# Eight rooms for expert weights, earlier rows of x, and six expert pairs combined by one-hot products

## The chip, the core and the metric

The kernel runs on one core of a Trainium2 chip. The metric is the device time of one execution in microseconds. All times inside an execution are counted from the start of the profiled span.

## What is computed

Two transformer blocks run one behind the other on 512 tokens of width 1024, in float32. The change lies in the second half of the first block, a mixture of 32 experts, and in the out projection in front of it:

```python
x = x + merged @ w_out
h2 = rmsnorm(x, norm2_g)
# router: best of 4 groups, then the best 2 of its 8 experts, gates from two softmaxes
# each token goes to 2 experts:
hid = silu(xb @ w_gate[e]) * (xb @ w_up[e])      # 1024 -> 256, twice
y   = (hid @ w_down[e]) * gate                   # 256 -> 1024
x = x + sum over the token's two experts of y
```

All 32 experts' weights (100.7 MB) have to be read from memory once.

## The kernel before

**Stages.** `window` computes the first block's mixer and, in `outproj`, the new x, block of 128 features by block (`X[:, d]`, d = 0 to 7). `moe` does the experts. `l0`, `ffn`, `l1`, `ffn` are the second block. Each engine works through its instructions in the order in which they were written.

**Rows.** The experts gather tokens by row, so x has to be in memory as rows (`hrows`). `Moe.row` (line 1683) turns one feature block by four TensorE transposes, copies it on ScalarE and writes 256 KB from ScalarE's queue. For d below `DROWS` (4) this is done in the out projection, a few matmuls behind the block; for the others in `route` (line 1709), in front of the routing's small matrix products.

**Pairs.** The experts are handled in 16 pairs (`NP`), 64 slots for each expert, 128 rows for a pair. A pair p takes: `gather` of its rows by POOL, `turn` (line 1888: eight transposes, then VectorE's multiplication by the gain), `gu` (line 1900: 32 matmuls from two weight pieces of 2 MB each, the gate and up products), `turn_hid`, and `down` (line 1926: 16 matmuls from a third piece). The loop runs `gu` of pair p and then `down` of pair o = p - 1.

**Combining.** Pairs below `NS` (12) are scattered: `down` writes one copy times the gate, `scatter` (line 1859) writes its rows to `yrows` in memory from POOL, and when the last of them has been written, `results` reads `yrows` back in four blocks of 128 tokens (1 MB each), two blocks at first and two when those have been added. `add_results` (line 1874) sums the two expert rows of each token on VectorE, transposes the sums on TensorE and adds them to X; it runs in the iterations o = 12 and o = 13, two blocks in each. The other four pairs are combined by one-hot products: `down` writes a copy and a correction to it (two operands), `spread` (line 1946) writes a matrix C with a one where token and slot meet, and `comb` (line 1951) multiplies, two pairs at a time, four matmuls of 128x512 for each d, and adds to X on VectorE. Pairs 12 and 13 are combined in pieces of two d in the iterations of pairs 14 and 15, pairs 14 and 15 in the last stage (`lastcomb`, lines 2136 on), between the first matmuls of `l0`.

**Rooms.** A weight piece is loaded into a room as soon as the room is free and its turn has come; `moe_jobs` (line 1581) writes down which piece goes into which room, `Core._dma` (line 90) issues, from SP's queue. Rooms are: ring 2, the two slabs (`esH`, `esL`); ring 1, two tiles `ew`; ring 0, `raw`; ring 3, one tile `ey`; ring 4, four `t` tiles of 256 KB; ring 5, the split-weight tiles `wh` and `wl`, four each; ring 6, two tiles of 512 KB. Five pieces are issued in the out projection, one at the start of `moe`, and three from ScalarE's queue behind the gates. In the steady state seven rooms turn round.

Of the kernel before, what the change touches and what calls it, by code (L numbers as in the profile page):

```python
# [8 lines left out]
F32 = mybir.dt.float32  # L9
F32R = mybir.dt.float32r  # L10
# [28 lines left out]
class Core:  # L39


    def __init__(self, ctx, tc, aps):
        self.tc, self.nc, self.a = tc, tc.nc, aps
        self.ctx = ctx
        self.const = ctx.enter_context(tc.tile_pool(name="const", bufs=1))
        self.slab = ctx.enter_context(tc.tile_pool(name="slab", bufs=1))
        self.wp = ctx.enter_context(tc.tile_pool(name="wp", bufs=1))
        self.xs = ctx.enter_context(tc.tile_pool(name="xs", bufs=1, side="right"))
        self.wr = ctx.enter_context(tc.tile_pool(name="wr", bufs=1, side="right"))
        self.tmp = ctx.enter_context(tc.tile_pool(name="tmp", bufs=1, side="right"))  # L50
        self.ps = ctx.enter_context(tc.tile_pool(name="ps", bufs=1, space=bass.MemoryType.PSUM))
        self.dram = ctx.enter_context(tc.tile_pool(name="dr", bufs=1, space=bass.MemoryType.DRAM))
        self.jobs = []
        self.groups = []
        self.n_dma = 0
        raw = lambda: self.wr.tile([128, 2048], F32, name="raw", tag="raw", bufs=NRAW)
        self.rings = [[raw, NRAW, 0], None, None, None, None, None, None]
        self.n_split = 0
        self.cur = 0
        self.turns = 0  # L60
        self.now = 0
        self.blk_off = 0
# [1511 lines left out]
NP = 16  # L1574
CAP = 64
NI = 12
NS = 12
DROWS = 4


def moe_jobs(c):

    gs = {}
    order = moe_order()

    def piece(i, *ring):
        n = order[i]
        w = c.a["e_w"][n // 3]
        o = 2 * (n % 3)
        if len(ring) == 1:  # L1590
            gs[n] = c.add_job(w[o:o + 2].rearrange("e p n -> p e n"), [(4096, 1)], split=False, ring=ring[0])
        else:
            gs[n] = sum((c.add_job(w[o + e], [(2048, 1)], split=False, ring=ring[e]) for e in range(2)), [])

    rooms = [(2,), (3,), (2,), (1,), (1,), (0, 0), (0, 4)]
    piece(0, 2)
    piece(4, 2)
    yield
    for i, ring in ((5, (1,)), (6, (1,)), (7, (0, 0)), (2, (6, 6)), (1, (5, 5)), (3, (3,)), (8, (0, 4))):
        piece(i, *ring)  # L1600
    for i in range(9, len(order)):
        ring = rooms.pop(0)
        if ring == (3,) and i > order.index(3 * NS + 3):
            ring = rooms.pop(0)
        rooms.append(ring)
        piece(i, *ring)
    for n in order:
        c.groups += gs[n]
    yield
# [13 lines left out]
class Moe:  # L1623
# [319 lines left out]
            nc.scalar.activation(Y[0][:, sl], acc, AF.Copy, scale=gate)  # L1943
            nc.vector.scalar_tensor_tensor(Y[1][:, sl], acc, gate, Y[0][:, sl], op0=OP.mult, op1=OP.subtract)

    def spread(self, idc, last):
        C = self.c.t512(F32R) if last else self.c.wp.tile([128, T], F32R, name="C", tag="wh", bufs=NSPL)
        self.c.nc.vector.tensor_scalar(C, self.iota, idc, None, op0=OP.is_equal)
        return C

    def comb(self, X, d, slots):
# [56 lines left out]

        return self.pool2.tile([128, 4096], F32, name="ey", tag="y0")

    def quarters(self):
        return Row([self.pool2.tile([128, D], F32, name="eq", tag="yq", bufs=4) for _ in range(2)])


def moe(c, X, nn, next_g):
    nc = c.nc
    c.mark("moe")
    m = c.moe
    m.pool2 = c.pool(m.es, "moe2")
    c.rings[3] = [m.early, 1, 0]  # L2020
    c.rings[6] = [m.quarters, 2, 0]
    c._dma()
    m.route(X)

# [12 lines left out]

    gather = lambda p: m.gather(m.idg[:, p:p + 1], p)
    xg = {}
    for p in range(2):  # L2040
        onehot(p, 1)
        slots(p)
        xg[p] = gather(p)
    m.gates()
    c.rings[4] = [lambda: Row([c.t512() for _ in range(4)]), 1, 0]
    turns = iter(("wh", "wl"))

    def halves():
        tag = next(turns)
        return Row([c.wp.tile([128, SPL], F32, name="we", tag=tag, bufs=NSPL) for _ in range(4)])  # L2050

    c.rings[5] = [halves, 2, 0]
    c._dma(queue=nc.scalar)
    xt = {0: m.turn(xg.pop(0))}
    slots2(0)
    slots2(1)
    C = {}
    Y = {}
    held = []

    def w():

        release()
        j, r = c.take_raw()
# [11 lines left out]
    comb = lambda q, d: m.comb(X, d, [(Y[q], C[q]), (Y[q + 1], C[q + 1])])  # L2076
    c.mark("experts")
    onehot(2)
    ht = {}
    for p in range(NP + 1):  # L2080
        if p < NP:
            hd = m.gu(xt.pop(p), w, m.rs[:, p:p + 1])
            release()
        if p == 0:
            slots(2)
            slots2(2)
        if p + 2 < NP:
            xg[p + 2] = gather(p + 2)
        if p + 1 < NP and p < 1:
            xt[p + 1] = m.turn(xg.pop(p + 1))  # L2090
        o = p - 1
        q = (o // 2 - 1) * 2
        ds = [] if q < NS else list(range(4)) if o % 2 == 0 else list(range(4, 8))
        for d in ds[:2]:
            comb(q, d)
        if o >= 0:
            tile = lambda dt: m.pool2.tile([128, D], dt, name="y", tag="yq", bufs=4)
            if o == NS:
                y = m.pool2.tile([128, 4, D], F32R, name="y4", tag="y0")
            if o < NS:  # L2100
                Y[o] = (tile(F32),)
            elif o < NP - 2:
                Y[o] = (y[:, 2 * (o - NS)], y[:, 2 * (o - NS) + 1])
            else:
                Y[o] = (tile(F32R), tile(F32R))
            m.down(ht.pop(o), w(), m.gate[:, o:o + 1], Y[o])
            release()
            if o < NS:
                m.scatter(o, Y[o][0])
            if o == NS - 1:  # L2110
                rooms = (lambda: Row([c.wp.tile([128, SPL], F32, name="yr", tag="wh", bufs=NSPL) for _ in range(4)]),
                         lambda: Row([tile(F32), tile(F32)]))
                res = [m.results(i, rooms[i]()) for i in range(2)]
            if o >= NP - 2:
                C[o] = m.spread(m.idc[:, o:o + 1], True)
        if 1 <= p < NP - 1:
            xt[p + 1] = m.turn(xg.pop(p + 1))
        for d in ds[2:]:
            comb(q, d)
        if p < NP:  # L2120
            ht[p] = m.turn_hid(hd)
        if o in (NS, NS + 1):
            b = 2 * (o - NS)
            for i in range(2):
                m.add_results(X, b + i, res[i])
            if o == NS:
                res = [m.results(2 + i, rooms[i]()) for i in range(2)]
            else:
                for q in (NS, NS + 1):
                    C[q] = m.spread(m.idc[:, q:q + 1], False)  # L2130
        if 1 <= p < 7:
            slots(2 * p + 2)
            slots2(2 * p + 2)
        if p < 6:
            onehot(2 * p + 4)
    m.beyond(X)
    c.mark("lastcomb")
    nn = c.norm_begin(next_g)
    accs = [c.bank(), c.bank()]
    c._split(c.cur + 1)  # L2140
    c._lows()
    for d in range(NB + 2):
        if d < NB:
            comb(NP - 2, d)
        if 1 <= d <= NB:
            nn[3](d - 1, X[:, d - 1])
            nc.sync.dma_start(c.xdr[:, d - 1], X[:, d - 1])
        if d >= 2:
            for acc in accs:
                for _ in c.block(1, *nn[:2], acc, first=d == 2, last=d == NB + 1, x0=d - 2):  # L2150
                    pass
    m.es.close()
    return nn[:3], accs
# [169 lines left out]
```

## Time and profile before

| | us |
|---|---|
| median of three runs | 1871.73 (1870.38 to 1872.22) |
| the profiled execution | 1871.83 |
| its span | 1870.0 |
| TensorE busy in the span | 1777.3 (95%) |
| VectorE busy | 1041.5 (56%) |
| ScalarE busy | 718.8 (38%) |
| POOL busy | 359.4 (19%) |

The busy shares are means over stages that have different limits; the stretch from about 290 to 650 us is the one that the change touches, and it is to be read by itself. In the rows below, PE is TensorE's matmuls, PEld its weight loads, DVE is VectorE, ACT is ScalarE, and SPq and ACTq are DMA issues from SyncE's and ScalarE's queues. An arrow in brackets names what ended the idle time in front of an instruction.

### The profile page before, as it was taken

To read this page: it belongs to the slowest core of one execution; us is meant where nothing else is said; L and a number is where in the kernel's file an instruction comes from. 1 tells how busy PE (TensorE), PEld (TensorE's weight loads), DVE (VectorE), ACT (ScalarE), POOL (GpSimd) and SP (SyncE) were. 2 spreads that over 40 slices of the span, in tenths; PEclk is the share of its full clock that TensorE was granted. 3 is DMA by queue.
4 is the path that set the end of the run, shared out by engine and by line. 5 is a ranking of instruction groups with operands and counts; after the bars stand their busy time and mean duration, and the time that the engine had idled before them with its cause. 6 is when DMAs were issued, how large, how long until landed. Compare 5 with 4: busy or idle time off the path is not lost.

```text
span 1870.0 us, 23372 instructions
## 1 busy us (share of the span) xinstructions
PE 1777.3 (95%) x8722; PEld 1326.1 (71%) x8722; DVE 1041.5 (56%) x1915; ACT 718.8 (38%) x1418; POOL 359.4 (19%) x392
## 2 busy tenths in 40 slices
PE   8999999799786999999999999999999999999998
PEld 6777787533233686667888888878777788888887
DVE  5765446543113767765655555564776565555555
ACT  6444334211000456664433333333666443333334
POOL 3212012111111251001211111121444221111111
PEclk9999999799997999999999999999999999999999
DMA  6124346599999320202322322243221322222321
GB/s 246 68 65 162 135 156 236 186 399 421 422 422 416 99 94 26 77 29 85 113 90 91 112 90 91 104 127 119 76 60 57 103 100 96 107 90 92 111 91 46
DMA packets 71831, 266.99 MB, mean 143 GB/s; under 512 B 24561, under 2 KB 31089, under 8 KB 46752
## 3 DMA queue, kind: packets, MB, share of 16 engines
q1 hardware_dynamic: 55120, 229.51, 33.2%
q0 software_dynamic: 9936, 27.47, 4.3%
q10 hardware_dynamic: 6656, 8.45, 1.3%
q8 instruction: 72, 1.18, 0.3%
q14 instruction: 47, 0.39, 0.1%
HBM read 251.57 MB, written 18.87 MB: 145 GB/s over the span
## 4 chain that ended last, share of the span: by engine, by line
PE 56%; DVE 6%; ACT 3%; issue 1%; DMA 0%; POOL 0%; POOLq 0%; DVEq 0%; ACTq 0%
PE psacc L227 15%; PE psacc L229 15%; PE psacc L228 15%; PE psT L709 2%; PE psO L861 2%; DVE wl L134 1%; PE psT L341 1%; PE psO L1440 1%; PE psS L1497 1%; PE psS L227 1%; PE psS L1185 1%; ACT wh L125 1%; PE psS L228 1%; PE psS L229 1%; ACT p L696 1%
## 5 line engine op out<-in xcount | busy, mean ns | idle before, releaser
L134 DVE TENSOR_TENSOR wl<-raw,wh 128x512 fp32r<-128x512 f32 x466 | 402.7, 867 | 246.3 <-ACT wh L125 244.8
L227 PE MATMUL psacc<-xh,wh 128*128 128x512 f32 x1008 | 407.4, 404 | 6.6 <-ACT wh L125 6.0
L125 ACT CAST wh<-raw 128x512 fp32r<-128x512 f32 x466 | 285.5, 617 | 321.6 <-PE psacc L228 272.4
L228 PE MATMUL psacc<-xl,wh 128*128 128x512 f32 x1008 | 394.6, 391 | 1.6 <-DVE xl L251 1.6
L229 PE MATMUL psacc<-xh,wl 128*128 128x512 f32 x1008 | 394.7, 392 | 0.1
L227 PEld LDWEIGHTS psacc<-xh,wh 128*128 128x128 f32 x1008 | 190.0, 189 | 56.0 <-issue 14.2
L229 PEld LDWEIGHTS psacc<-xh,wl 128*128 128x128 f32 x1008 | 189.8, 188 | 41.5 <-DVE wl L134 0.6
L228 PEld LDWEIGHTS psacc<-xl,wh 128*128 128x128 f32 x1008 | 190.3, 189 | 35.7 <-DVE xl L251 3.2
L227 PE MATMUL psacc<-uh,wh 128*128 128x512 f32 x480 | 187.0, 390 | 2.6 <-DVE x L453 2.6
L229 PE MATMUL psacc<-uh,wl 128*128 128x512 f32 x480 | 186.8, 389 | 0.0
L228 PE MATMUL psacc<-ul,wh 128*128 128x512 f32 x480 | 186.7, 389 | 0.0
L421 POOL TENSOR_TENSOR t<-t,rstd 128x512 f32<-128x512 f32 x64 | 82.9, 1295 | 526.6 <-ACT t L420 526.6
L453 DVE TENSOR_TENSOR x<-psacc,x 128x512 f32<-128x512 f32 x120 | 82.7, 689 | 125.4 <-PE psacc L229 125.4
L227 PEld LDWEIGHTS psacc<-uh,wh 128*128 128x128 f32 x480 | 90.1, 188 | 22.3 <-issue 3.8
L379 POOL TENSOR_TENSOR ss<-ss,t 128x512 f32<-128x512 f32 (+1 forms) x49 | 58.5, 1193 | 234.9 <-ACT t L372 234.6
L229 PEld LDWEIGHTS psacc<-uh,wl 128*128 128x128 f32 x480 | 90.1, 188 | 18.9
L228 PEld LDWEIGHTS psacc<-ul,wh 128*128 128x128 f32 x480 | 90.1, 188 | 18.5
L243 ACT CAST uh<-t 128x512 fp32r<-128x512 f32 x64 | 39.7, 621 | 131.3 <-DVE t L422 131.3
L709 PE MATMUL psT<-cst,p 128*128 128x128 f32 x448 | 77.1, 277 | 13.4 <-ACT p L696 12.6
L709 PEld LDWEIGHTS psT<-cst,p 128*128 128x128 f32 x448 | 55.2, 140 | 42.6 <-ACT p L696 22.6
L420 ACT ACTIVATE t<-psacc 128x512 f32<-128x512 f32 x64 | 38.3, 599 | 80.8 <-PE psacc L229 80.8
L1914 DVE SCALAR_TENSOR_TENSOR hd<-psS,rs,sl 128x256 f32<-128x256 f32 x16 | 7.7, 484 | 107.9 <-ACT sl L1913 107.9
(493 smaller groups left out, 2707.7 us busy)
## 6 DMA issues: line engine op xcount, KB each, us to landing
raw<-ffn SPq DMA_DIRECT2D x64, 1024.0 KB
ew<-e_w SPq DMA_DIRECT2D x14, 2048.0 KB
raw<-e_w SPq DMA_DIRECT2D x17, 1024.0 KB
esH<-e_w SPq DMA_DIRECT2D x7, 2048.0 KB
esL<-e_w SPq DMA_DIRECT2D x7, 2048.0 KB
ey<-e_w SPq DMA_DIRECT2D x5, 2048.0 KB
raw<-w_in_a SPq DMA_DIRECT2D x8, 1024.0 KB
raw<-od_qk SPq DMA_DIRECT2D x8, 1024.0 KB
```

The lines of the kernel that those rows point to most:

```text
L125: nc.scalar.copy(h[:, :n], r)
L134: self.nc.vector.tensor_sub(l, r, h)
L227: nc.tensor.matmul(acc, wh, xh, start=first, stop=False)
L228: nc.tensor.matmul(acc, wh, xl, start=False, stop=False)
L229: nc.tensor.matmul(acc, wl, xh, start=False, stop=last)
L243: nc.scalar.copy(h, src)
L379: self.nc.gpsimd.tensor_add(s, s, q)
L420: nc.scalar.activation(r, acc, AF.Relu)
L421: nc.gpsimd.tensor_mul(r2, r, st["r2"])
L453: nc.vector.tensor_add(X[:, d], acc, X[:, d])
L709: nc.tensor.transpose(t[:, o:o + 128], p[:, m * 128:m * 128 + 128], c.ident)
L861: self.c.nc.tensor.matmul(o[64 * hh:64 * hh + 64], self.V[:, kb, v:v + 64], pt[hh][:, kb], start=kb == 0, stop=kb == 3, skip_group_check=True)
```

## The change

- `moe_jobs` has eight rooms that turn round. New are a ring of four `wh` tiles with one of two 512 KB tiles `yw` (rings 7 and 6), used up to the piece of pair 9's down product; ring 3 is used up to pair 11's second piece. Each room that consists of quarters or halves is issued as four or two DMAs.
- Five pieces are issued in the out projection as before, and at the start of `moe` two (pieces 1 and 6 of the order) where there was one. Two are issued from ScalarE's queue behind the gates where there were three.
- `DROWS` is 7: the rows of d = 4, 5 and 6 are turned and written in the out projection, d = 7 alone in `route`.
- `NS` is 10. The reads of the results start behind pair 9, `add_results` runs at o = 11 and o = 13. Pairs 10 to 15 are combined by one-hot products: 10 and 11 in front of `down` of pair 12, 12 and 13 in front of `down` of pair 14, each with all eight d in one go; 14 alone in front of `down` of pair 15; 15 alone in `lastcomb`.
- `spread` is called directly behind `down` of each of these pairs, and writes into the tiles `rstd` and `ss`, or a `t` tile for the last two.

```diff
-        self.rings = [[raw, NRAW, 0], None, None, None, None, None, None]
+        self.rings = [[raw, NRAW, 0], None, None, None, None, None, None, None, None]
-NS = 12
-DROWS = 4
+NS = 10
+DROWS = 7
 def moe_jobs(c):
-    rooms = [(2,), (3,), (2,), (1,), (1,), (0, 0), (0, 4)]
+    rooms = [(2,), (2,), (1,), (1,), (0, 0), (7, 6), (3,), (0, 4)]
+    last = {(7, 6): order.index(3 * NS - 1), (3,): order.index(3 * NS + 4)}
     piece(0, 2)
-    piece(4, 2)
+    piece(2, 2)
     yield
-    for i, ring in ((5, (1,)), (6, (1,)), (7, (0, 0)), (2, (6, 6)), (1, (5, 5)), (3, (3,)), (8, (0, 4))):
+    for i, ring in ((3, (1,)), (4, (1,)), (5, (0, 0)), (1, (8, 5)), (6, (7, 6)), (7, (3,)), (8, (0, 4))):
         piece(i, *ring)
     for i in range(9, len(order)):
-        ring = rooms.pop(0)
-        if ring == (3,) and i > order.index(3 * NS + 3):
-            ring = rooms.pop(0)
-        rooms.append(ring)
-        piece(i, *ring)
+        while i > last.get(rooms[0], i):
+            rooms.pop(0)
+        rooms.append(rooms.pop(0))
+        piece(i, *rooms[-1])
...
-    def spread(self, idc, last):
-        C = self.c.t512(F32R) if last else self.c.wp.tile([128, T], F32R, name="C", tag="wh", bufs=NSPL)
-        self.c.nc.vector.tensor_scalar(C, self.iota, idc, None, op0=OP.is_equal)
+    def spread(self, p):
+        c = self.c
+        C = c.t512(F32R) if p >= NP - 2 else c.tmp.tile([128, T], F32R, name="C", tag=("rstd", "ss")[p % 2], bufs=1)
+        c.nc.vector.tensor_scalar(C, self.iota, self.idc[:, p:p + 1], None, op0=OP.is_equal)
         return C
...
 def moe(c, X, nn, next_g):
-    c.rings[3] = [m.early, 1, 0]
-    c.rings[6] = [m.quarters, 2, 0]
+    quarters = lambda tag: Row([c.wp.tile([128, SPL], F32, name="we", tag=tag, bufs=NSPL) for _ in range(4)])
+    c.rings[5] = [lambda: quarters("wl"), 1, 0]
+    c.rings[6] = [lambda: m.half("yw"), 1, 0]
+    c.rings[7] = [lambda: quarters("wh"), 1, 0]
+    c.rings[8] = [lambda: m.half("yq"), 1, 0]
     c._dma()
     m.route(X)
...
     m.gates()
+    c.rings[3] = [m.early, 1, 0]
...
-        q = (o // 2 - 1) * 2
-        ds = [] if q < NS else list(range(4)) if o % 2 == 0 else list(range(4, 8))
-        for d in ds[:2]:
-            comb(q, d)
+        if o == NP - 1 or o >= NS + 2 and o % 2 == 0:
+            for d in range(NB):
+                comb((o - 1,) if o == NP - 1 else (o - 2, o - 1), d)
...
             if o < NS:
                 m.scatter(o, Y[o][0])
+            else:
+                C[o] = m.spread(o)
             if o == NS - 1:
...
                 res = [m.results(i, rooms[i]()) for i in range(2)]
-            if o >= NP - 2:
-                C[o] = m.spread(m.idc[:, o:o + 1], True)
...
-        for d in ds[2:]:
-            comb(q, d)
-        if o in (NS, NS + 1):
-            b = 2 * (o - NS)
+        if o in (NS + 1, NS + 3):
+            b = o - NS - 1
...
         if d < NB:
-            comb(NP - 2, d)
+            comb((NP - 1,), d)
```

## Rows read from the trace of the kernel before

**Rows 1.** The page's slices: GB/s in 40 equal parts of the span.
```profile
GB/s 246 68 65 162 135 156 236 186 399 421 422 422 416 99 94 26 77 29 85 113 90 91 112 90 91 104 127 119 76 60 57 103 100 96 107 90 92 111 91 46
```

**Rows 2.** Windows by stage: stretch, its length, busy us by engine, PEclk, DMA share, GB/s.
```profile
364.89:457.00 92.11, 87.05 (x507) 34.45 (x506) 34.64 (x102) 11.34 (x21) 13.35 (x14) 0.98 1.00 407
468.95:545.39 76.44, 58.80 (x265) 21.01 (x265) 10.38 (x18) 6.98 (x14) 9.88 (x10) 0.96 1.02 421
545.39:627.00 81.61, 64.31 (x272) 28.11 (x273) 28.96 (x46) 10.25 (x18) 8.66 (x14) 0.84 0.80 330
...
627.00:648.40 21.40, 19.77 (x80) 14.79 (x81) 20.60 (x23) 12.65 (x22) 10.89 (x8) 1.00 0.45 149
```

**Rows 3.** Timeline: start, length, engine, line; the down product of pair 11.
```profile
545.39 3.68 PE L1934 MATMUL psacc<-esH,ht 128*64 128x512 f32 x8 [4.18 <-DMA esH<-e_w]
548.83 2.61 PE L1934 MATMUL psO<-esH,ht 128*64 128x512 f32 x8
```

**Rows 4.** TensorE's waits from 364 to 627 us: total, times, longest.
```profile
PE psT L1884 <- DVE yr L1879: 7.1, 3, 5.6
```

**Rows 5.** Timeline: the two steps of add_results and what starts behind them.
```profile
561.23 2.23 POOL L1870 DMA_DIRECT2D yr<-yrows  x4 [7.22 <-DMA yrows<-y,dest]
...
566.50 0.44 PE L1921 MATMUL psT<-cst,hd 128*128 128x128 f32 x2 [1.14 <-DVE xt L1896]
...
571.67 0.69 DVE L1879 TENSOR_TENSOR yr<-yr 128x512 f32<-128x512 f32 x1 [4.62 <-DMA yr<-yrows]
...
581.51 5.06 PE L1908 MATMUL psS<-ew,xt 128*64 128x512 f32 x16
...
595.64 0.44 PE L1921 MATMUL psT<-cst,hd 128*128 128x128 f32 x2 [1.18 <-DVE xt L1896]
...
601.45 5.33 PE L1908 MATMUL psS<-esH,xt 128*64 128x512 f32 x16
606.62 3.60 PE L1908 MATMUL psS<-esL,xt 128*64 128x512 f32 x16
```

**Rows 6.** Windows at the second step of add_results, columns as in rows 2.
```profile
596.00:600.00 4.00, 1.73 (x11) 1.29 (x11) 3.79 (x7) 0.37 (x1) 0.00 (x0) 0.75 1.01 424
600.00:604.00 4.00, 4.00 (x14) 1.89 (x14) 2.26 (x5) 0.00 (x0) 0.00 (x0) 0.50 1.01 424
```

**Rows 7.** Windows in the out projection and around routing, columns as in rows 2.
```profile
328.00:344.00 16.00, 15.89 (x75) 12.68 (x73) 6.25 (x8) 3.07 (x6) 2.70 (x3) 1.00 0.00 0
...
344.00:392.00 48.00, 35.38 (x207) 17.23 (x209) 25.81 (x105) 8.18 (x15) 6.66 (x9) 0.79 0.87 318
```

**Rows 8.** Timeline: one block of rows in the out projection, and the first gather.
```profile
314.71 0.60 PE L1688 MATMUL psT<-cst,x 128*128 128x128 f32 x4
315.06 0.48 PE L227 MATMUL psacc<-mh,wh 128*128 128x512 f32 x1
...
357.29 1.10 POOL L1854 DMA_INDIRECT xg<-hrows,idg  x1 [16.88 <-DVE oh L1814]
```

**Rows 9.** Timeline of SP's queue: issues of two weight pieces that follow each other.
```profile
384.82 0.38 SPq L104 DMA_DIRECT2D ey<-e_w  x1
388.26 0.37 SPq L104 DMA_DIRECT2D esL<-e_w  x1
```

**Rows 10.** Timeline: combination, down product of pair 14, its evacuation, the last combination.
```profile
610.14 2.12 PE L1958 MATMUL psS<-C,y 128*128 128x512 f32 x8
612.19 1.94 PE L1934 MATMUL psacc<-ew,ht 128*64 128x512 f32 x8
613.96 1.89 PE L1934 MATMUL psO<-ew,ht 128*64 128x512 f32 x8
...
616.62 0.75 DVE L1944 SCALAR_TENSOR_TENSOR y<-psO,gate,y 128x512 fp32r<-128x512 f32 x1 [0.97 <-ACT y L1943]
617.29 0.48 DVE L1948 TENSOR_SCALAR t<-mc,idc 128x512 fp32r<-128x512 f32 x1
...
627.00 3.03 PE L1958 MATMUL psS<-t,y 128*128 128x512 f32 x12 [1.42 <-DVEq L1968]
```

More of the change, by code (lines that the diff above doesn't have):

```diff
@@ L2009, in early, with half @@
         return self.pool2.tile([128, 4096], F32, name="ey", tag="y0")
-    def quarters(self):
-        return Row([self.pool2.tile([128, D], F32, name="eq", tag="yq", bufs=4) for _ in range(2)])
+    def half(self, tag):
+        return Row([self.pool2.tile([128, D], F32, name="eh", tag=tag, bufs=2) for _ in range(2)])
 def moe(c, X, nn, next_g):
@@ L2044, in moe @@
     m.gates()
+    c.rings[3] = [m.early, 1, 0]
     c.rings[4] = [lambda: Row([c.t512() for _ in range(4)]), 1, 0]
[L2046 to L2052, printed above, removed]
     c._dma(queue=nc.scalar)
@@ L2074, in release @@
             c._free(held.pop(0))
-    comb = lambda q, d: m.comb(X, d, [(Y[q], C[q]), (Y[q + 1], C[q + 1])])
+    comb = lambda qs, d: m.comb(X, d, [(Y[q], C[q]) for q in qs])
     c.mark("experts")
@@ L2091, in moe @@
         o = p - 1
-        q = (o // 2 - 1) * 2
-        ds = [] if q < NS else list(range(4)) if o % 2 == 0 else list(range(4, 8))
-        for d in ds[:2]:
-            comb(q, d)
+        if o == NP - 1 or o >= NS + 2 and o % 2 == 0:
+            for d in range(NB):
+                comb((o - 1,) if o == NP - 1 else (o - 2, o - 1), d)
         if o >= 0:
-            tile = lambda dt: m.pool2.tile([128, D], dt, name="y", tag="yq", bufs=4)
-            if o == NS:
+            tile = lambda dt, tag: m.pool2.tile([128, D], dt, name="y", tag=tag, bufs=2)
+            if NS <= o < NP - 2 and o % 2 == 0:
                 y = m.pool2.tile([128, 4, D], F32R, name="y4", tag="y0")
             if o < NS:
-                Y[o] = (tile(F32),)
+                Y[o] = (tile(F32, "yq"),)
             elif o < NP - 2:
-                Y[o] = (y[:, 2 * (o - NS)], y[:, 2 * (o - NS) + 1])
+                Y[o] = (y[:, 2 * (o % 2)], y[:, 2 * (o % 2) + 1])
             else:
-                Y[o] = (tile(F32R), tile(F32R))
+                Y[o] = tuple(tile(F32R, ("yq", "yw")[o % 2]) for _ in range(2))
             m.down(ht.pop(o), w(), m.gate[:, o:o + 1], Y[o])
@@ L2109, in moe @@
                 m.scatter(o, Y[o][0])
+            else:
+                C[o] = m.spread(o)
             if o == NS - 1:
-                rooms = (lambda: Row([c.wp.tile([128, SPL], F32, name="yr", tag="wh", bufs=NSPL) for _ in range(4)]),
-                         lambda: Row([tile(F32), tile(F32)]))
+                rooms = (lambda: quarters("wh"), lambda: m.half("yw"))
                 res = [m.results(i, rooms[i]()) for i in range(2)]
-            if o >= NP - 2:
-                C[o] = m.spread(m.idc[:, o:o + 1], True)
         if 1 <= p < NP - 1:
             xt[p + 1] = m.turn(xg.pop(p + 1))
-        for d in ds[2:]:
-            comb(q, d)
         if p < NP:
             ht[p] = m.turn_hid(hd)
-        if o in (NS, NS + 1):
-            b = 2 * (o - NS)
+        if o in (NS + 1, NS + 3):
+            b = o - NS - 1
             for i in range(2):
                 m.add_results(X, b + i, res[i])
-            if o == NS:
+            if b == 0:
                 res = [m.results(2 + i, rooms[i]()) for i in range(2)]
-            else:
-                for q in (NS, NS + 1):
-                    C[q] = m.spread(m.idc[:, q:q + 1], False)
         if 1 <= p < 7:
```

## The prediction

> **What bounds the kernel now.** I read the slices of the page first. DMA moves 399 to 422 GB/s in slices 9 to 13 and under 250 in all others [rows 1], so the change lies in the one stretch where the expert weights are streamed. Then the table by stage [rows 2] splits that stretch. From 364.9 to 457 us TensorE is busy 87.1 of 92.1 us: it is the bound there (eight pairs at about 13.1 us). From 469 to 545.4 it is busy only 58.8 of 76.4 us, while DMA runs at a share of 1.02 and 421 GB/s: the weights are late, and every pair waits for a piece. From 545.4, where the down product of pair 11 starts, to 627.0, where the last combination starts, DMA falls off and TensorE is busy 64.3 of 81.6 us at a mean clock of 0.84. So neither of the two bounds that last part; the waits and the timeline say what does.
>
> The down product of pair 11 waited 4.18 us for its weights and ran at the lower clock, 6.05 us in all [rows 3]. Later TensorE waits 7.1 us in front of the transposes of the scattered results [rows 4], and the timeline has the chain: POOL waited 7.22 us for the last scatter before it could read `yrows` at 561.23, and the first sum on VectorE came at 571.67, after 4.62 us of waiting for that read [rows 5]. TensorE ended pair 13's `turn_hid` at 566.94 and began pair 14 at 581.51: 14.6 us for one `add_results` step (two blocks). The second such step, with its data there, took from 596.08 to 601.45, 5.4 us [rows 5]. Nine microseconds of stall are what there is to win here.
>
> **Rooms and rows, ahead of routing.** Between 328 and 344 us DMA is idle (share 0.00), and over 344 to 392 it moves 318 GB/s instead of 420 [rows 7]. After 392 it is never idle until the tail, so whatever lead it has at 392 it keeps. Two things set this lead.
> - Three more rows are transposed in the out projection, where TensorE is busy 15.89 of 16 us [rows 7]. Four transposes take 0.35 us there (314.71 to the next matmul at 315.06) [rows 8]; three rows cost 1.1 us, and routing starts later by that. They save nothing behind it: the first gather was released by VectorE's one-hot, not by the row writes [rows 8]. Their 256 KB writes fall into the idle DMA stretch.
> - The two pieces now issued in front of routing (4.2 MB instead of 2.1) keep DMA busy until about 356 us; but what follows is limited by rooms that come free. With one room more, each later piece is issued one release earlier; releases are 3.4 us apart (384.82 to 388.26) [rows 9]. So the lead is 3.4 - 1.1, less about 0.3 us for the smaller transfers: I take 2.0 us. Bounds: -1.1 us (only the delay of routing is left) and 5.0 us (a whole piece, 2.1 MB at 0.42 MB/us).
>
> The issues moved: ACT loses eight issues behind the gates and SP gets twelve in place of four behind the out projection. At 0.38 us for an issue [rows 9] twelve are 4.6 us; SP's next issue waits for pair 0's first piece to be used up, far behind that, so this is hidden. POOL keeps its gathers there.
>
> The stream of 469 to 545 us contains rooms of four 256 KB tiles already, and still runs at 421 GB/s [rows 2]. The Trainium skill, page "Perfetto Trace Analysis", section "DMA Optimizations", speaks against cutting pieces into quarters: larger DMAs saturate HBM better, small ones pay an overhead per transfer. With the figures of "DMA: Bandwidth & Descriptors", section "Bandwidth" (341 GB/s for 1 MB, 425 for 16 MB), the 3.1 MB more that go in quarters would cost 1.8 us, an estimate; the row decides for less.
>
> **Scatters and the reads of the results.** Pair 10 is not scattered before 545 us: 0.26 MB less (half of 2048 slots are filled by 1024 assignments), 0.6 us. Pair 11's scatter came later. But the first half of the result reads, 2.1 MB, is now issued behind pair 9, some 25 us ahead of where pair 11's weights land, into a saturated stream: 5.0 us at 0.42 MB/us. Bounds: 0 (the reads fill gaps) and 5.0; I take 5.0, since the share there is 1.02 [rows 2].
> The down product of pair 11 then starts at 545.4 - 2.0 - 0.6 + 5.0 = 547.8, 2.4 us later.
>
> **The tail, from there to the last combination** (81.6 us before). TensorE works in order, and from here on the weights come sooner than it uses them, so each microsecond added counts.
> - Combinations. Before: four groups of eight matmuls, 2.1 us each [rows 10], 8.3 us in the loop. After: pairs 10/11 and 12/13 with 32 matmuls each; eight took 2.12 us and twelve 3.03, so each further one 0.23, and 2.12 + 24 x 0.23 = 7.6 us, and pair 14 alone, which stands directly behind its own down product: it must wait for the second half's copy, its correction (0.75 us) and C (0.48 us), ready 1.95 us after TensorE's end (615.85 to 617.77), of which 0.4 us is covered by a transpose; its 16 matmuls then go at the pace of the VectorE additions (0.69 us each [rows 5], through three banks), 4.7 us [rows 10]. Sum 7.6 + 7.6 + 6.3 = 21.5: **+13.2**.
> - Evacuation. Pair 11 now gets a correction as pairs 12 and 13 had (0.75), and the one-hot C of pairs 11, 12 and 13 (0.48 each) is made in front of `turn` on VectorE, for which TensorE waits: **+2.2**. The cover is gone, since nothing else is left for TensorE there.
> - Results. Both steps find their data there (read 25 us ahead): 2 x 5.4 in place of 14.6 + 5.4: **-9.2**.
> - Pair 11's down product at the full clock, 3.7 us as in [rows 10], in place of 6.05: **-2.4** (bounds -2.4 and 0). The 1.4 and 1.7 us that pairs 14 and 15 lose to the clock behind their `add_results` steps I keep, for pairs 13 and 15: at 600 to 604 the granted clock was 0.50, the lower level (1.2 GHz), behind 4 us in which TensorE was busy 1.73, and pair 15's first half took 5.33 us where its second took 3.60 [rows 5, 6].
> - End. Before, 1.4 us behind the last group of eight [rows 10]; after, the copy, correction and C of pair 15, 1.95 us as above, and some 0.35 us for the branch, an estimate: **+0.9**.
> Sum +4.7, and 2.4 from before it: the last combination starts 7.1 us later. In it, half of the combination's matmuls are gone (16 x 0.23 = 3.7 us), but VectorE is busy 20.60 of 21.40 us there [rows 2]: I take -0.5 (bounds -3.7 and 0). **Total +6.6 us**; the profiled execution took 1871.83 us (median 1871.73), so **1878.4 us**. All behind 648 us only shifts.
>
> **Rivals.**
> - *The reads cost the weights nothing.* If POOL's reads take only time that the weight queue leaves over, pair 11's down product starts at 542.8 and the total is +1.6: **1873.4, not slower**. It decides if that product starts before about 544. For it: the weights are queued several pieces ahead. Against: 421 GB/s with a share of 1.02 leave nothing over, and the reads at 561 took 10.4 us from issue to the first sum [rows 5], so they do share. Chance 0.16.
> - *The clock stays up.* The pairs behind `add_results` run at the upper level (2.4 GHz), -3.1: **1875.3**. For it: the 14.6 us stall is gone. Against: the second step had no stall and the clock fell all the same [rows 6]. The Trainium skill, "TensorE: Matmul & The Clock Gate", section "HAM oscillation — how this bites in real kernels", says that waits between bursts of matmuls drop the clock and that a loop without them keeps it; by that this rival should win. Chance 0.08.
> - *The change does not do what it says*: the eighth room gives no lead (routing 1.1 us later, DMA waits for rooms all the same) and pair 11 still waits at the lower clock: +3.1 + 2.4: **1883.9**. Chance 0.11.
> - *Faster*: reads free, clock up and a whole piece of lead (-5.0 - 3.1 - 3.0): **1867.3**. Chance 0.15, since these help each other: an earlier pair 11 leaves shorter waits.
> - *The forecast*, 1875.6 to 1881.5: chance 0.50.
>
> **How the numbers follow.** 0.2% (3.7 us) is about what a measurement of this kernel can tell from no change: the same is 1868.1 to 1875.6. Slower: 0.50 + 0.11 = 0.61; same 0.16 + 0.08 = 0.24; faster 0.15. The range goes from 1867, which takes in the faster case, to 1884.
>
> **What would show it.** In the profile after: DMA near 420 GB/s from 344 to 356 us; no wait of TensorE for the sums of the results; the down product of pair 11 at 546 to 550 us; four blocks of combination matmuls, 7.6 us twice, in the loop; the last combination at 633 to 636; low clock behind both result steps. I am wrong if pair 11 comes before 544, if TensorE still waits for weights in pairs 13 to 15, or if the last combination becomes shorter than 20 us.

## The result and the profile after

| | before | after |
|---|---|---|
| median, us | 1871.74 | 1888.76 (1886.89 to 1890.63) |
| ratio | | 1.0092 [1.0075, 1.011] |
| the profiled execution | 1871.83 | 1890.63 |
| its span | 1870.0 | 1888.9 |

Slower by 17 us; 6.6 were forecast, and the range ended at 1884. The profiled execution of after is the longest of its four. 3.2 us of its 18.8 lie in code that the change doesn't touch: TensorE's first matmuls behind 34 us are 1.65 us later than before, and another 1.5 us are lost at 1485 us, both times in a stretch at a lower granted clock (0.89 from 26 to 36 us, 0.79 from 1482 to 1490; before had 1.00 at both places of its program). All positions of after below are therefore 1.65 us late. The windows (columns as in [rows 2]) show the first of the two, after and then before:

```profile
26.00:36.00 10.00, 8.30 (x37) 6.63 (x36) 5.35 (x7) 4.69 (x11) 6.67 (x6) 0.89 0.44 178
```
```profile
26.00:36.00 10.00, 9.76 (x47) 7.89 (x46) 6.94 (x9) 5.91 (x14) 5.94 (x4) 1.00 0.42 173
```

The stages of after, as in [rows 2, 7]:

```profile
344.00:392.00 48.00, 25.68 (x157) 13.11 (x157) 23.21 (x93) 4.96 (x10) 5.63 (x7) 0.72 0.77 263
374.07:466.20 92.13, 87.04 (x507) 34.48 (x506) 34.69 (x102) 11.32 (x21) 13.30 (x14) 0.98 0.94 375
478.21:551.00 72.79, 57.41 (x266) 20.95 (x265) 11.04 (x19) 7.23 (x15) 12.22 (x15) 0.98 1.01 418
551.00:644.00 93.00, 74.93 (x321) 37.70 (x321) 41.68 (x65) 11.24 (x20) 4.38 (x7) 0.91 0.70 289
644.00:665.10 21.10, 18.88 (x64) 13.35 (x65) 19.76 (x23) 12.70 (x22) 10.07 (x8) 0.84 0.45 150
```

Around routing DMA moves 263 GB/s where it moved 318, although two pieces go ahead instead of one. The first eight pairs take the same 92.1 us, but start 9.2 us later (374.07 instead of 364.89), 7.5 of them without the 1.65. The stage that waits for weights is shorter by 3.6 us (72.8 instead of 76.4), and the tail takes 93.0 us in place of 81.6.

The timeline has the reason for the late start (columns as in [rows 3]):

```profile
353.87 6.11 SPq L101 DMA_DIRECT2D eh<-e_w  x2
360.58 1.10 POOL L1854 DMA_INDIRECT xg<-hrows,idg  x1 [17.67 <-DVE cm L1767]
361.12 0.38 ACTq L104 DMA_DIRECT2D ey<-e_w  x1
361.54 0.48 ACTq L104 DMA_DIRECT2D raw<-e_w  x1
362.06 3.76 ACTq L101 DMA_DIRECT2D t<-e_w  x4
371.16 1.94 PE L1894 MATMUL psT<-cst,xg 128*128 128x128 f32 x8 [11.31 <-DMA xg<-hrows,idg]
```

From the gather's issue to TensorE's first transpose of it are 10.6 us; before, with the issue at 357.29 [rows 8], 4.7. SyncE's twelve issues dragged on until 359.98, and ScalarE, which before was busy with eight small issues for 4.3 us, now puts a whole 2 MB piece and 1 MB of another into the queues 0.5 to 1 us behind the gather. The DMA packets in the traces show what this does: before, the gather's 128 packets of 4 KB took 2.4 us, with 0.1 MB of other packets among them; in after they took 6.7 us, among 1.56 MB of ScalarE's pieces.

The tail, line by line: pair 11's down product with a wait in its middle, the first block of each step of sums, one combination of two pairs, pair 14's, and the end:

```profile
551.00 1.04 PE L1934 MATMUL psacc<-raw,ht 128*64 128x512 f32 x2
554.67 1.50 PE L1934 MATMUL psacc<-raw,ht 128*64 128x512 f32 x5 [2.64 <-DMA raw<-e_w]
...
562.17 1.55 PE L1884 MATMUL psT<-cst,we 128*128 128x128 f32 x8 [0.85 <-DVE we L1879]
...
575.37 7.73 PE L1959 MATMUL psS<-C,y 128*128 128x512 f32 x32
...
604.03 1.94 PE L1884 MATMUL psT<-cst,we 128*128 128x128 f32 x8 [0.85 <-DVE we L1879]
...
630.36 5.51 PE L1959 MATMUL psS<-t,y 128*128 128x512 f32 x16 [1.69 <-DVE t L1949]
...
637.57 1.89 PE L1934 MATMUL psO<-ew,ht 128*64 128x512 f32 x8
644.00 1.33 PE L1959 MATMUL psS<-t,y 128*128 128x512 f32 x4 [4.54 <-DVEq L1969]
```

The sums find their data there (no stall as in [rows 4, 5]), each block of 32 matmuls takes the 7.7 us that were forecast, and the last combination waits 4.54 us where [rows 10] had 1.42.

### The profile page after: what moved, and what is told of

It reads as the page before. It is cut to its first block, busy times and chain, and to the rows that moved or that the text cites. A ratio compares the mean times of both kernels' runs of the same rounds, so it can differ in the third digit from the quotient of the medians.

```text
span 1888.9 us, 23513 instructions
## 1 busy us (share of the span) xinstructions
PE 1785.5 (95%) x8754; PEld 1334.9 (71%) x8754; DVE 1052.9 (56%) x1935; ACT 720.0 (38%) x1420; POOL 355.3 (19%) x390
## 4 chain that ended last, share of the span: by engine, by line
PE 56%; DVE 6%; ACT 2%; issue 1%; DMA 0%; POOL 0%; DVEq 0%; POOLq 0%; ACTq 0%
PE psacc L227 15%; PE psacc L229 15%; PE psacc L228 15%; PE psT L709 2%; PE psO L861 1%; DVE wl L134 1%; PE psT L341 1%; PE psO L1440 1%; PE psS L227 1%; PE psS L1497 1%; PE psS L1185 1%; PE psS L228 1%; PE psS L229 1%; ACT p L696 1%; ACT wh L125 1%
## 5 line engine op out<-in xcount | busy, mean ns | idle before, releaser
L229 PEld LDWEIGHTS psacc<-uh,wl 128*128 128x128 f32 x480 | 90.1, 188 | 18.8
## 6 DMA issues: line engine op xcount, KB each, us to landing
esH<-e_w SPq DMA_DIRECT2D x7, 2048.0 KB, 13.2
```

The source lines that it names most:

```text
L229: nc.tensor.matmul(acc, wl, xh, start=False, stop=last)
```

## Experiments

"End of pair 11" is the end of its down product (before 551.4, after 558.3 less the 1.65); "end of stage" is the first matmul of line 301 behind the last combination (before 648.4, after 665.2 less the 1.65). In the other kernels what the profile is early or late by at 305 us (-0.3 to 1.3) is taken off; the lines are shown as they stand. Executions of one kernel spread over 1 to 6 us, and a profiled one lies anywhere in that, so times are compared by medians and places by the profile. The kernel before ran beside each group: 1872.15 to 1872.39. The kernel after did not; beside its own runs before had 1871.74, so differences from after can be 0.6 us off.

A place at the end of pair 11 says less in the kernels with the old rooms than in those with the new. Three of the runs below (late sums, sums inside pair 14, one sum inside) have the instructions of before up to there, and yet their down product of pair 11 waits and runs so:

```profile
544.94 1.94 PE L1934 MATMUL psacc<-esH,ht 128*64 128x512 f32 x8 [1.71 <-DMA esH<-e_w]
```
```profile
545.30 1.94 PE L1936 MATMUL psacc<-esH,ht 128*64 128x512 f32 x8 [1.69 <-DMA esH<-e_w]
```
```profile
545.90 3.68 PE L1936 MATMUL psacc<-esH,ht 128*64 128x512 f32 x8 [4.32 <-DMA esH<-e_w]
```

It ends at 547.6, 547.6 and 552.3, where before had 551.4. So "earlier than before" at this place is not resolved below 4 us. Three kernels with the new rooms that are the same up to there but for the padding (after, pair 14 in the last stage, VectorE padded) end it at 556.2 to 556.7, so a comparison with after is good to half a microsecond.

### One piece ahead (edit of after)
```diff
-    c.rings[6] = [lambda: m.half("yw"), 1, 0]
-    c.rings[7] = [lambda: quarters("wh"), 1, 0]
     ...
     m.gates()
+    c.rings[6] = [lambda: m.half("yw"), 1, 0]
+    c.rings[7] = [lambda: quarters("wh"), 1, 0]
     c.rings[3] = [m.early, 1, 0]
```


> The changed kernel, but piece 6 is issued by ScalarE behind the gates; only piece 1 is issued ahead of routing, as before. In the changed kernel the first gather took 10.6 us from its issue to TensorE's first transpose (before 4.7). Theory A (the second piece, still arriving when the gather runs, holds it up): the gather lands in about 5 us, the first gate product starts 5 to 6 us earlier (368 instead of 374), the down product of pair 11 about 3 to 4 us earlier, the time about 1885. Theory B (the pieces that ScalarE now issues a little behind the gather are what holds it up): the gather still takes 9 to 11 us and the time stays at 1888 to 1889. Theory C (early pieces do pay for themselves later): the gather is faster, but the down product of pair 11 comes no earlier, time 1888 or more.

1884.35 us (1883.47 to 1885.47), 4.4 less than after. The gather, issued at 358.73, is transposed 4.6 us later, and the wait in front now ends with VectorE, not with DMA:

```profile
358.73 1.10 POOL L1854 DMA_INDIRECT xg<-hrows,idg  x1 [17.45 <-DVE oh L1814]
359.80 1.80 ACTq L101 DMA_DIRECT2D we<-e_w  x4
361.64 0.98 ACTq L101 DMA_DIRECT2D eh<-e_w  x2
362.97 0.39 ACTq L104 DMA_DIRECT2D ey<-e_w  x1
363.36 1.94 PE L1894 MATMUL psT<-cst,xg 128*128 128x128 f32 x8 [4.54 <-DVE Gf L1806]
```

End of pair 11 at 552.3, 4.4 earlier. But the edit also puts six small issues in front of ScalarE's 2 MB piece, so it doesn't tell A from B; the next run does.

### ScalarE's pieces held (edit of after)
```diff
+    nc.scalar.copy(m.small("hold", 8), xg[0][:, :8])
     c._dma(queue=nc.scalar)
```


> The changed kernel, but ScalarE copies eight columns of the first gathered tile before it issues its weight pieces, so these start only when the gather has landed. Theory A (SyncE's second piece holds the gather up): still 8 us or more from issue to landing, and since the weights then start later, the time grows by 1 to 4 us. Theory B (ScalarE's pieces hold it up): the gather lands in about 5 us, the first gate product starts near 368, time 1885 to 1888, since about 5 us of weight stream are given away in front.

1885.04 us (1880.62 to 1885.91), 3.7 less. Both pieces go ahead on SyncE, and yet the gather lands in 5.5 us:

```profile
358.90 1.10 POOL L1854 DMA_INDIRECT xg<-hrows,idg  x1 [17.69 <-DVE st L1824]
364.41 0.20 ACT L2052 COPY hold<-xg 128x8 f32<-128x8 f32 x1 [4.69 <-DMA xg<-hrows,idg]
364.52 1.94 PE L1894 MATMUL psT<-cst,xg 128*128 128x128 f32 x8 [5.97 <-DMA xg<-hrows,idg]
```

So the large pieces issued right behind the gather take most of the 5.9 us (theory B). The other runs agree: in the five kernels with these pieces right behind it the gather took 9.7 to 10.6 us from its issue to TensorE's first transpose, in the nine others 4.5 to 5.6. Pair 11 ends at 550.3, 6.4 earlier than in after. Against before it is 1.1 earlier, less than this place resolves; whether the eighth room gave a lead is not shown by it.

### Before with seven rows
```diff
-DROWS = 4
+DROWS = 7
```


> The kernel before with seven rows turned in the out projection instead of four, nothing else. My term: routing starts 1.1 us later and nothing is saved behind it. Read from the changed kernel's trace: 1.3 us. Theory A: the first gather is issued 1.1 to 1.6 us later, the lead of the stream shrinks by as much, time 1873 to 1874. Theory B (three copies and three writes less on ScalarE's queue in front of the gates shorten routing by as much): 1872, no change.

1873.62 us (1871.17 to 1874.70), ratio 1.0005 [0.9996, 1.0014] and 1.3 us by the medians; in the profile the first gather is issued at 359.26, 1.4 us later than before when 0.5 us that it is late at 305 us are taken off. The interval holds 1, no change; the place agrees with theory A and with the 1.1 of the prediction.

### Reads later (edit of after)
```diff
-            if o == NS - 1:
+            if o == NS + 1:
...
-        if o in (NS + 1, NS + 3):
-            b = o - NS - 1
+        if o in (NS + 2, NS + 3):
+            b = 2 * (o - NS - 2)
```


> The changed kernel, but the results are read two pairs later (behind the down product of pair 11) and added behind pairs 12 and 13; the combination stays ten scattered and six by one-hot products. My forecast's term (reads in the saturated stream cost the weights 5.0 us): the down product of pair 11 starts at 546 instead of 551 and the time falls by 4 to 5 us, to 1884. Rival (the reads take only what the weight queue leaves over): pair 11 within 1 us of the changed kernel, time 1888 to 1889.

1891.13 us (1890.43 to 1892.30), 2.4 **more**, or at any rate not less. Both theories missed it. The term itself was there: pair 11 ends at 552.9, 3.8 earlier, so the reads had cost the weights 3.8 of the 5.0 us. But behind it:

```profile
564.04 5.95 PE L1908 MATMUL psS<-esH,xt 128*64 128x512 f32 x16 [4.90 <-DMA esH<-e_w]
```

The first half of the results is now read behind pair 11, and TensorE waits 4.9 us for the second piece of pair 13, for which it did not wait in after. What the weights gained in front is lost there: moving bytes inside a full stream moved the wait here.

### Twelve pairs scattered (edit of after)
```diff
-NS = 10
+NS = 12
...
-        if o in (NS + 1, NS + 3):
-            b = o - NS - 1
+        if o in (NS + 1, NS + 2):
+            b = 2 * (o - NS - 1)
```


> The changed kernel with twelve pairs scattered and four combined by one-hot products again, but the results are added one pair later than in the kernel before (behind pairs 13 and 14). Rooms, rows and early pieces as in the changed kernel. By my terms: one block of combination matmuls less (-7.7), two corrections and two C less (-2.5), both result steps with their data there (0), reads of results out of the weight stream (0 to -5.0). So 1874 to 1879; the price of the six one-hot pairs is 10 to 15 us. Rival (the results are late again and the stall of the kernel before returns): TensorE waits 4 us or more for the first sums, 1881 to 1886.

1886.04 us (1882.55 to 1888.04), only 2.7 less, and my sum of 10 to 15 was wrong. The time is the rival's, but not for its reason: all waits for sums together are 3.0 us. TensorE's timeline:

```profile
565.23 3.25 PE L1934 MATMUL psacc<-esH,ht 128*64 128x512 f32 x8 [3.04 <-DMA esH<-e_w]
...
578.29 3.65 PE L1908 MATMUL psS<-ew,xt 128*64 128x512 f32 x16 [1.51 <-DMA ew<-e_w]
585.57 3.32 PE L1934 MATMUL psacc<-ew,ht 128*64 128x512 f32 x8 [3.62 <-DMA ew<-e_w]
```

With one block of combination less, TensorE waits 8.2 us for the weights of pairs 12 and 13. After had 7.7 us of combination in this place. The weights are the bound here, not TensorE.

### Before with late sums
```diff
-        if o in (NS, NS + 1):
-            b = 2 * (o - NS)
+        if o in (NS + 1, NS + 2):
+            b = 2 * (o - NS - 1)
...
-                for q in (NS, NS + 1):
-                    C[q] = m.spread(m.idc[:, q:q + 1], False)
...
+            if o >= NS:
+                C[o] = m.spread(m.idc[:, o:o + 1], ("rstd", "ss")[o % 2] if o < NP - 2 else None)
```


> The kernel before with one edit: the results are added behind pairs 13 and 14 instead of 12 and 13 (C of pairs 12 and 13 lies in rstd and ss, so that it doesn't need the rooms of the results). My prediction counted the 9 us stall in front of the sums as time to win. Theory A (the stall is on the path): the time falls by 7 to 9 us, to 1863 to 1865. Theory B (the stall lay beside the weight stream, which runs at a share of 1.01 until 605 us; without it TensorE waits for the weights of pairs 13 and 14 instead, as it did for 8.2 us in the run with twelve pairs scattered, and the second step of sums now lies behind the end of the stream): the waits for weights from 545 us on grow by 4 to 8 us and the time is 1870 to 1875.

1869.01 us (1867.02 to 1872.19), ratio 0.9987 [0.9978, 0.9996]: faster than both kernels, by 3.3 us, not by 9. The stall of [rows 4, 5] is gone. TensorE's waits from 545 to 640 us (total, times, longest) show what came in its place:

```profile
PE psT L1884 <- DVE yr L1879: 2.3, 2, 1.5
PE psS L1908 <- DMA raw<-e_w: 2.3, 1, 2.3
PE psacc L1934 <- DMA ew<-e_w: 1.7, 1, 1.7
PE psacc L1934 <- DMA esH<-e_w: 1.7, 1, 1.7
PE psS L1908 <- DMA esL<-e_w: 1.5, 1, 1.5
...
PE psacc L1934 <- DMA t<-e_w: 1.0, 2, 0.8
PE psacc L1934 <- DMA raw<-e_w: 0.2, 1, 0.2
```

8.4 us of waits for weights, where before had 4.5 (4.2 and 0.3). That is theory B's reason, with a growth of 3.9 just under its 4 to 8, and a time 1 us under its range.

### Pair 14 in the last stage (edit of after)
```diff
-        if o == NP - 1 or o >= NS + 2 and o % 2 == 0:
+        if o >= NS + 2 and o % 2 == 0:
             for d in range(NB):
-                comb((o - 1,) if o == NP - 1 else (o - 2, o - 1), d)
+                comb((o - 2, o - 1), d)
...
-            comb((NP - 1,), d)
+            comb((NP - 2, NP - 1), d)
```


> The changed kernel, but pair 14 is combined together with pair 15 in the last stage, as in the kernel before, not by itself in front of pair 15's down product. Its own block took 7.2 us of TensorE's time (1.7 of waiting and 5.5). Theory A (the last stage is bound by VectorE, so that 16 matmuls more cost nothing there): 6 to 7 us less, about 1882. Theory B (the last stage grows by the 16 matmuls, 3.7 us): 3 to 4 us less, about 1885.

1882.23 us (1881.56 to 1882.57), 6.5 less, as theory A has it; but its reason holds only in part. From the last combination to the end of the stage it takes 23.3 us instead of 21.2. That is paid for by the end of the loop:

```profile
632.72 3.03 PE L1959 MATMUL psS<-t,y 128*128 128x512 f32 x12 [2.15 <-DVEq L1969]
```

2.15 us instead of 4.54 (forecast 2.3). The difference is VectorE's sequencer. Its records for the branch of line 1969, here and then in after (instruction, count, duration in ns, start):

```profile
L1969 DVEq COMPARE_BRANCH  x1: 72/72/72, 632.0 to 632.0; - x1
L1969 DVEq EVENT_SEMAPHORE  x1: 21/21/21, 632.5 to 632.5; - x1
```
```profile
L1969 DVEq COMPARE_BRANCH  x1: 72/72/72, 640.9 to 640.9; - x1
L1969 DVEq EVENT_SEMAPHORE  x1: 21/21/21, 643.8 to 643.8; - x1
```

From the branch to the next instruction: 0.5 us here, 2.9 in after.

### VectorE padded (edit of after)
```diff
+    pad = m.small("pad", 8)
+    for _ in range(48):
+        nc.vector.memset(pad, 0.0)
```


> The changed kernel with 48 tiny extra VectorE instructions behind routing, in time that VectorE has free; nothing else. In the changed kernel VectorE's first instruction behind the branch in front of the last stage came 2.9 us after the branch; in the kernel before and in the run with twelve pairs scattered 0.5 to 0.6 us. Theory A (it depends on where VectorE's code lies when the branch comes, which every added instruction moves): the gap changes to 0.5 to 1 us, the last combination starts 2 us earlier against pair 15's down product, time 1886 to 1887. Theory B (the gap comes from what the changed kernel does there, the copy and C of pair 15 coming last): the gap stays at 2.9 us, time 1888 to 1889.

1888.36 us (1887.62 to 1891.17); the gap stays at 2.9 us (branch at 638.1, next instruction at 641.0).

Theory A, in this form, falls. Theory B isn't shown either: the run with twelve pairs scattered has the same last steps and a gap of 0.6. A rival that no run tests is a wait for instructions: the traces show two loads of 8 KB of instructions within 1.2 us behind the branch in after, but they show the same two in the run with pair 14 in the last stage, whose gap is 0.5. The cause of these 2.4 us stays open.

### Three parts undone (edit of after)
One piece ahead and pair 14 in the last stage, with the diffs above, and:
```diff
-DROWS = 7
+DROWS = 4
```


> The changed kernel with three of its parts undone together: one piece ahead of routing (alone: -4.4 us), four rows (alone, seen from the kernel before: -1.3), pair 14 combined in the last stage (alone: -6.5). What is left of the change are the eight rooms and ten pairs scattered, six by one-hot products. Theory A (the three prices stand on the path one behind the other and add up): 1876.5 (1875 to 1878), and the rooms with the six one-hot pairs cost the 4 us that are left. Theory B (they cover each other: an earlier first gather only makes TensorE wait for weights later): 1879 or more.

1876.78 us (1873.48 to 1878.41): -12.0, against -12.2 from the three prices added up. Theory A. What is left, eight rooms with ten pairs scattered and six by one-hot products, costs 4.5 us against before (ratio 1.0024 [1.0015, 1.0034]). Its profiled execution is the shortest of the ten: the stage ends at 648.4, at the same time as before. So it doesn't show where the 4.5 are; that stays open.

### All together
Seen from after: ScalarE's pieces held, four rows, twelve pairs scattered with the sums behind pairs 13 and 14, the combination's portions as in the kernel before.
```diff
-DROWS = 7
+DROWS = 4
-NS = 10
+NS = 12
...
+    nc.scalar.copy(m.small("hold", 8), xg[0][:, :8])
...
+        q = (o // 2 - 1) * 2
+        ds = [] if q < NS else list(range(4)) if o % 2 == 0 else list(range(4, 8))
...
-            comb((NP - 1,), d)
+            comb((NP - 2, NP - 1), d)
```


> A kernel built from what the runs showed: rooms and two early pieces of the changed kernel; ScalarE's pieces held until the first gather has landed; four rows in the out projection; twelve pairs scattered, pairs 12 and 13 combined in portions of two blocks as in the kernel before, 14 and 15 in the last stage; the results added behind pairs 13 and 14. Theory (the stream of weights sets the time up to 605 us, and eight rooms give it 4 to 7 us of lead once the gather is not held up): pair 11's down product starts at 538 to 541 instead of 545.4, no stall in front of the sums, the last combination starts at 612 to 620 instead of 627, time 1858 to 1866. Rival (the rooms give no lead): pair 11 at 545 or later, time 1870 or more.

1874.25 us (1872.41 to 1878.08), ratio 1.0014 [1.0005, 1.0023]; the time is the rival's. Pair 11 starts its down product at 543.2, between the two theories. Behind it no lead is left: the down product of pair 13 starts at 582.0 (with 3.63 us of waiting for `ew`), where the late sums in the kernel before had it at 577.1. Two things stand against it. First, the rows. With two pieces ahead, the writes of four rows run beside SyncE's second piece:

```profile
352.46 4.35 SPq L101 DMA_DIRECT2D eh<-e_w  x2
354.66 0.37 ACTq L1691 DMA_DIRECT2D hrows<-t  x1
355.08 0.21 ACT L1772 ACTIVATE eg<-eg 128x16 f32<-128x16 f32 x1 [2.17 <-DMA hrows<-t]
...
355.99 0.15 DVE L1826 TENSOR_SCALAR idg<-idc 128x1 int32<-128x1 f32 x1
...
360.13 1.10 POOL L1854 DMA_INDIRECT xg<-hrows,idg  x1 [20.01 <-DVE rcol L1801]
```

The list of tokens was there at 356.1, the gather was issued 4.0 us later; before, 0.8 (356.5 to 357.29). The profile names VectorE's `rcol` as what released it, which a gather doesn't read; what it does need is the rows in memory, and ScalarE itself had waited 2.17 us for one of these writes. The packets in the traces settle it: the last packet of the rows landed at 358.83, 1.30 us ahead of the gather's issue. In all seven kernels with two early pieces the gather was issued 1.30 to 1.38 us behind that packet; in the seven others the rows had been there for 1.46 us or more, and it was issued 0.83 us behind the list. So the last row write held it. Four rows and two early pieces don't go together: 3.2 us more than the 0.83; with one piece (the run with three parts undone) the gather was issued at 357.70. In after, with the list there at 358.91, the rows cost 0.8 us in the same way. Second, the stream is slower with the eight rooms: from 392 to 545 us it moved 420 GB/s in all five kernels with the old rooms, and 416 to 419 in the nine with the new. The packets agree with that: medians of 84, 159 and 309 ns for 2, 4 and 8 KB from 400 to 540 us, so that a byte in quarters takes 9% longer and one in halves 3%. 0.7% of 153 us is 1.1 us.

### Sums inside pair 14 (edit of before with late sums)
```diff
         for h in range(2):
+            if h and mid:
+                mid()
             ws = w()
...
+            mid = lambda: [m.add_results(X, i, res[i]) for i in range(2)]
```


> The kernel before with the late sums of the run before_late_sums, but the first two blocks of results are added between the two halves of pair 14's gate products, where TensorE waited 2.3 us for a weight piece and then about 1.2 us for the halves of pair 13's down product. Theory (from 570 to 584 us TensorE waits for the stream, so a step put there costs only what exceeds the waits; the results have landed at 571.7): pair 15's gate products start at 587 to 590 instead of 593.1, the last combination at 617 to 620 instead of 623.05, time 1864 to 1867. Rival (the last pieces aren't there by then, the wait moves on to pair 15): 1868 to 1870, with new waits for weights of 3 us or more behind 584.

1869.39 us (1866.66 to 1872.28): nothing over the late sums. The rival's time, but not the wait that it named: the first block's sums were there at once, the second block's were not:

```profile
571.43 1.22 PE L1884 MATMUL psT<-cst,yr 128*128 128x128 f32 x8
579.38 1.94 PE L1884 MATMUL psT<-cst,y 128*128 128x128 f32 x8 [6.73 <-DVE y L1879]
```

### One sum inside
The same with the first block alone there (`mid = lambda: m.add_results(X, 0, res[0])`), the second at its later place.

> The kernel before with the late sums, and only the first block of results added between the halves of pair 14's gate products (its data was there at 571.4 in the run sums_inside_pair14, the second block's came 6.7 us too late for that place). Theory (the wait of 2.3 us for the weight piece covers most of this step): pair 15's gate products start at 590.5 to 592 instead of 593.1, time 1866.5 to 1868. Rival (the down product of pair 13 then waits for its halves, which land at 580 to 581.5 in any case): 1868.5 to 1869.5, no gain over the late sums alone.

1870.46 us (1868.64 to 1872.45), the rival or worse: no gain. With the sums inside, TensorE comes to the second piece of pair 15 earlier and waits for it (both sums inside, then one):

```profile
597.11 3.65 PE L1910 MATMUL psS<-esL,xt 128*64 128x512 f32 x16 [0.52 <-DMA esL<-e_w]
```
```profile
597.10 3.65 PE L1910 MATMUL psS<-esL,xt 128*64 128x512 f32 x16 [1.63 <-DMA esL<-e_w]
```

The late sums alone start on it at 597.08 without a wait. So with the sums inside, the last weights set the time at this place, and nothing is gained. Neither of these two kernels is shown to be better than the late sums alone.

## Why the prediction was wrong

The direction was right, and so were most durations. In the profiled execution 15.1 us were lost between 50 us and the end of the stage, against 6.6 forecast:

| stretch | forecast | measured |
|---|---|---|
| to the end of pair 11's down product | 0.0 (+2.4 at its start, -2.4 clock) | +5.2 |
| from there to the last combination | +7.1 | +10.1 |
| last stage | -0.5 | -0.3 |

The split between the first two stretches hangs on where the profiled execution of before ended pair 11, and is good to about 4 us; the sum is not touched by that. The last stage came near by luck in part: half of its combination matmuls were gone, as forecast, but its granted clock was 0.84 where [rows 2] had 1.00.

- **Rooms and rows: the step that failed.** "The issues moved ... this is hidden. POOL keeps its gathers there." The issues were priced by their duration on their own queue (0.38 us [rows 9]), and nothing was priced for what their bytes do to the gather. In [rows 8] the gather of before went out alone, with ScalarE's small issues 1.1 us behind it, and took 4.7 us up to its use; I did not ask what would be in flight beside it in after. It took 10.6, all of it on the path, since TensorE has nothing else to do there. Holding ScalarE's pieces gave 6.4 us back at the end of pair 11 (3.7 in the median), one piece less 4.4. The early pieces weren't in by 356 us either: from 345 to 357 us DMA moved 287 GB/s, not 420, and the last packet of SyncE's pieces landed at 363.05. Whether the 2.0 us of lead were right stays open. With ScalarE held, pair 11 ended 1.1 us before the kernel before, with 3.8 us of reads against it, which would make 4.9; against the late sums it ended 2.7 later, which would make 1.1.
- **Rows:** 1.1 forecast; 1.3 us seen from the out projection's end in after (345.91 instead of 342.95, less 1.65), 1.3 in the median of the run that has them alone, not resolved from zero there. "They save nothing behind it" was read from a trace with one piece ahead; with two, the kernel with everything together and four rows had 4.0 us between list and gather, and after, with seven, 1.7, where before had 0.8.
- **Early reads:** 5.0 forecast, 3.8 measured by moving them. The rival that they cost nothing is out.
- **Small transfers:** I let the row of 421 GB/s decide against the page and took 0.3 us. The nine kernels with the new rooms moved 0.7% less, 1.1 us over 153 us. The Trainium skill's section "DMA Optimizations" ("Perfetto Trace Analysis") has the right sign here. The estimate of 1.8 us from the Trainium skill, "DMA: Bandwidth & Descriptors", section "Bandwidth", was about as far off on the other side.
- **Pair 11 at the full clock, -2.4:** did not come. Its product again waits for a weight piece (2.64 us) and runs from 551.00 to 558.32, 7.3 us instead of 3.7. The prediction gives no reason for this term: the wait in front of it comes from the stream, and removing the stall behind it changes nothing there. The low clock of [rows 3] also belongs to that execution: behind waits of 1.71 and 1.69 us two kernels with the same instructions ran the product at the upper level.
- **Combination, +13.2:** 7.73, 7.74 and 7.2 (1.69 + 5.51) make 22.7 instead of 21.5.
- **Evacuation, +2.2:** TensorE's waits for `xt` behind pair 11 grew from 2.7 to 4.7 us, +2.0.
- **Results, -9.2:** two steps of 5.7 and 6.1 us instead of 5.4; the stall is gone. But "Nine microseconds of stall are what there is to win here" was wrong in itself. "From here on the weights come sooner than it uses them" holds only because TensorE stood still beside a stream with a share of 1.01 [rows 6]: late sums alone bring 3.3 us, and then the weights are waited for. In after the saved time was filled with 7.7 us of combination, which is why the sum came near and the reading was still wrong.
- **End, +0.9:** +3.1. 2.4 of it are VectorE's gap behind the branch, which no row of before shows.
- **Clock behind the sums:** pair 13's gate products took 8.43 us and pair 15's 7.78, pair 14's at the upper level 7.1: some of the loss was kept, as forecast, about 1 us less than before (8.49 and 8.77). Behind the sums the granted clock was near the lower level both times, though TensorE's longest wait inside these steps was 1.43 us:

```profile
567.00:570.00 3.00, 3.00 (x9) 0.98 (x10) 0.69 (x1) 0.00 (x0) 1.60 (x2) 0.54 1.02 421
609.00:611.00 2.00, 2.00 (x8) 0.65 (x8) 0.91 (x2) 0.00 (x0) 0.00 (x0) 0.57 0.86 356
```

The rival that the clock stays up is out.

The 3.2 us outside the stretch explain the profiled execution but not the median: the shortest of the four (1886.89) is still 2.9 above the range.

## What to carry to other kernels

A transfer that is brought forward is to be priced twice: by the queue that issues it, and by the small transfer on the path that will be in flight beside it; here a 512 KB gather took 10.6 us from issue to use with 3 MB issued right behind it, and 5.6 with these held. A stall is worth what it costs only if nothing else is late: ask what the other streams would be doing at the time that it gives back, and count from their last byte. And take a clock loss off a sum only if the change removes what stood in front of it.

## What the runs showed of the hardware

- The gather was issued 0.83 us behind its list, or 1.30 to 1.38 us behind the last packet of the row writes that it reads, whichever came later, in all fourteen kernels. With a second 2 MB piece beside these writes and four rows left to write, it went out 4.0 us behind its list.
- An indirect gather of 128 rows of 4 KB took 4.5 to 5.6 us from its issue to its use in the nine kernels without ScalarE's large pieces right behind it, and 9.7 to 10.6 in the five with them. Its packets took 2.4 us with 0.1 MB of others among them (before) and 6.7 with 1.56 MB (after).
- 2, 4 and 8 KB packets took 84, 159 and 309 ns in a full stream; the stream moved 420 GB/s with the old rooms, and 416 to 419 with one more room, of quarters and halves.
- VectorE went on 0.5 to 0.6 us behind the branch in nine kernels and 2.9 to 3.1 us in five; these five are the ones that combine pair 14 by itself with ten pairs scattered. 48 more VectorE instructions changed nothing; the cause is open.
